# Attention weights transposed by VectorE and a round trip through DRAM instead of by TensorE

## The chip, the cores and the metric

The kernel runs on one core of a Trainium2 chip. The metric is the device time of one execution in microseconds; before the change it is 685.24 us, the median of three runs (685.07 to 685.33). TensorE is called PE in the profile, VectorE DVE, ScalarE ACT, GpSimd POOL; SP is the engine that issues most transfers (DMA).

## The reference

One encoder layer over 1024 tokens of width 1024, in float32. The normalised and modulated input `u` goes through one combined input projection; two groups of eight heads of width 64 mix the tokens, each with its own rule for the weights; their outputs are gated, concatenated and projected back, and a residual and a layer norm end it.

```python
# forgetting attention (FoX), blocks of 128 queries
s = jnp.einsum('bhqd,bhkd->bhqk', q, k) * scale
s = s + (f_q[..., :, None] - f_k[..., None, :])
p = jax.nn.softmax(jnp.where(causal, s, -jnp.inf), axis=-1)
out = jnp.einsum('bhqk,bhkd->bhqd', p, v)

# stick-breaking attention
z = jnp.einsum('bhqd,bhkd->bhqk', q, k) * scale
log_keep = jnp.where(strict, jax.nn.log_sigmoid(-z), 0.0)
later = lax.cumsum(log_keep, axis=3, reverse=True) - log_keep
w = jnp.where(strict, jnp.exp(jax.nn.log_sigmoid(z) + later), 0.0)
out = jnp.einsum('bhqk,bhkd->bhqd', w, v)

y = concat(y_fox * silu(fg), y_sb * silu(sg)) @ w_out
x = layer_norm(alpha * x + gate * y, ln_g, ln_b)
```

## The kernel before

**Units and pairs.** The 16 heads are worked in eight pairs of two; pairs 0 to 3 are stick-breaking, 4 to 7 forgetting. A unit is `(p, h, i)`: pair, head of the pair, block of 128 queries. Block `i` sees `i + 1` key blocks of 128, so a unit's weights are 128 by `(i + 1) * 128`, 4.5 blocks or 576 columns in the mean. There are 128 units. Stick-breaking pairs take the blocks in rising order, forgetting pairs in falling order, and pair 7 alternates between its heads.

**Precision.** Matrix products run on float32 values rounded to TensorE's shorter float32 type, with the rest of the rounding in a second tile ("hi" and "lo"). Each operand of a product so needs a cast (hi) and a subtraction (lo = full minus hi).

**A unit's way.** `att_scores` computes the scores S (lines 427, 428) into one PSUM tile of two banks, of which there is one. In a stick-breaking unit ScalarE makes two sigmoids of it (447: `kp`, 448: `be`), VectorE runs one or two scans backwards over `kp` (453, 457), and POOL multiplies `be` by the shifted `kp` (461) and clears the last column (462). In a forgetting unit VectorE adds the forget row `fb` and reduces (434), ScalarE takes the exponential with its sum (440), VectorE the reciprocal (441), and POOL scales the row (442). `att_transpose` then transposes each 128 by 128 block on TensorE by the identity into a PSUM tile `T` of up to four blocks (478), ScalarE casts that to hi (480) and VectorE subtracts for lo (481). `att_pv` multiplies the transposed weights with the values for two query blocks at once (493); its output goes through ScalarE, VectorE and POOL (512 to 514) and SP stores it to `y_dr` (522).

**What sets the order.** TensorE's order is written by hand: iteration `k` of the last loop issues the scores of unit `k`, a share of the fillers, the product of a pair of units that became ready in the iteration before, the transposes of unit `k - LAG` (LAG = 2), and another share of the fillers. The fillers are the input projections of later pairs (lines 270 to 272 and 327 to 329), and towards the end the output projection (882 to 884). The other engines, SP among them, are ordered by the framework's scheduler; each of them works strictly in its order, so an instruction that waits holds up all behind it.

**Buffers.** `att` has six tiles of 128 by 1024, shared by `kp`, `be`, `a` and the forget rows `fb`; a stick-breaking unit takes two, a forgetting unit one. The transposed weights have three tiles each for hi and lo. Keys lie in `kst` (hi, with a copy made by a transfer, line 252) and `klo`.

Of the kernel before, what the change touches and what calls it, by code (L numbers as in the profile page):

```python
# [8 lines left out]
F32 = mybir.dt.float32  # L9
F32R = mybir.dt.float32r  # L10
AF = mybir.ActivationFunctionType
ALU = mybir.AluOpType
# [15 lines left out]
def tile_hybrid_layer(  # L28
# [216 lines left out]
    def evac_k(p, ch, acc, kst, klo, heads):  # L245
        s = slice(ch * 512, ch * 512 + 512)
        for h in heads:
            r = slice(h * HD, h * HD + HD)
            o = slice((1 - h) * HD, (1 - h) * HD + HD)
            first = nc.scalar.copy(kst[h][r, s], acc[r, :])  # L250
            kf = kst[h].bitcast(F32)
            nc.sync.dma_start(kf[o, s], kf[r, s])
            if p not in CASTS_FIRST:
                last = nc.vector.tensor_tensor(klo[r, s], acc[r, :], kf[r, s], op=ALU.subtract)
        if p in CASTS_FIRST:
            for h in heads:
                r = slice(h * HD, h * HD + HD)
                last = nc.vector.tensor_tensor(klo[r, s], acc[r, :], kst[h].bitcast(F32)[r, s], op=ALU.subtract)  # L258
        return first, last
# [106 lines left out]
    def forget_rows(lf):  # L366
# [16 lines left out]
        nc.scalar.copy(fr, ft)  # L383
        nc.sync.dma_start(f_dr.rearrange("h (t p) -> (h t) p", p=P), fr)
        yield
# [21 lines left out]
    def att_causal(u):  # L407
        p, h, i = u
        if p >= 4:
            f = fb[2 * (p - 4) + h]  # L410
            dg = slice(i * P, i * P + P)
            nc.vector.tensor_tensor(f[:, dg], f[:, dg], ps_causal[0][:, :P] if ps_causal else causal, op=ALU.add)

    def att_scores(u, following):
# [3 lines left out]
        ns = 1 if ke <= 512 else 2  # L418
        w = ke // ns
        qs = slice(i * P, i * P + P)  # L420
        dg = slice(ke - P, ke)
        if p >= 4:
            f = fb[2 * (p - 4) + h]
        S = s_tile(f"S_{p}_{h}_{i}")
        for s in range(ns):
            ks = slice(s * w, s * w + w)
            nc.tensor.matmul(S[:, s, :w], qst[p][h][:, qs], kst[p][h][:, ks], start=True, stop=False)  # L427
            nc.tensor.matmul(S[:, s, :w], z, klo[p][:, ks], start=False, stop=True)  # L428
        v3 = lambda a: a[:, :ke].rearrange("p (a b) -> p a b", a=ns)
        if p >= 4:  # L430
            a = att_tile(f"a_{p}_{h}_{i}")
            nm = sb.tile([P, 1], F32, tag="nm", bufs=4, name=f"nm_{p}_{h}_{i}")
            l = sb.tile([P, 1], F32, tag="l", bufs=4, name=f"l_{p}_{h}_{i}")
            rows = nc.vector.tensor_tensor_reduce(out=v3(a), in0=S[:, :ns, :w], in1=v3(f),  # L434
                                           op0=ALU.add, op1=ALU.min, scale=-1.0, scalar=BIG,
# [5 lines left out]
            nc.vector.reciprocal(l, l)  # L441
            nc.gpsimd.tensor_scalar(a[:, :ke], a[:, :ke], l, 1.0, op0=ALU.mult, op1=ALU.mult)  # L442
            st_w[u] = a
        else:
# [16 lines left out]
            nc.gpsimd.tensor_tensor(be[:, :ke - 1], be[:, :ke - 1], kp[:, 1:ke], op=ALU.mult)  # L461
            nc.gpsimd.memset(be[:, ke - 1:ke], 0.0)
            st_w[u] = be

    def att_transpose(u):
# [639 lines left out]
```

## Time and profile before

| | before |
|---|---|
| device time, median of three | 685.24 us |
| profiled execution | 685.25 us |
| its span, first to last instruction | 683.5 us |
| busy PE / DVE / ACT / POOL | 98% / 66% / 56% / 63% |
| transfers | 81.60 MB, mean 119 GB/s |

A row of groups reads: line, engine, operation, tile written <- tiles read, shapes, count | total busy us, mean ns of one | idle us of the engine just before, and what ended it. A row of the timeline reads: start in us, duration in us, engine, line, operation. A row of transfers ends with KB each and the median us from issue to landing; the `SPq` rows of the timeline are the time for which SP is held by issuing one. A row of windows gives, for a stretch, busy us of PE, PE's weight loads, DVE, ACT and POOL with their counts, the granted clock, and the share and rate of the transfers.

### The profile page before, as it was taken

Reading aid. Unit: us, or ns where it says so; the run is one execution under the profiler, and the core shown is the slowest. Engines: PE = TensorE matmul, PEld = TensorE weight load, DVE = VectorE, ACT = ScalarE, POOL = GpSimd, SP = SyncE. Lnnn points to the kernel's source line nnn. Section 1 sums busy time; section 2 is a strip of 40 time slices with the busy share of each in tenths; the row PEclk is TensorE's granted clock in tenths of the full one; section 3 lists DMA queues with packets and bytes.
Section 4 is the critical chain, followed back from the end, with each engine's and each line's share of the span. In section 5 each row is a group of like instructions: output and inputs, shape, how many; then the busy total and the mean of one; then the engine's idle time right before and its main releaser. Section 6 shows DMA issues by size and latency. Waiting matters only on the chain.

```text
span 683.5 us, 11770 instructions
## 1 busy us (share of the span) xinstructions
PE 667.2 (98%) x4021; PEld 587.2 (86%) x4021; DVE 450.6 (66%) x914; ACT 382.0 (56%) x861; POOL 427.7 (63%) x558
## 2 busy tenths in 40 slices
PE   5999999999999999999999999999999999999995
PEld 4789898888998888889988888899988889888885
DVE  6785368867666667676675665765566677774645
ACT  5668357856567666566675564655565667531000
POOL 5558977756348566556388896877584364665411
PEclk9999999999999999999999999999999999999999
DMA  9966231112102121122144563453341298143301
GB/s 338 410 236 233 82 105 44 41 29 60 29 9 86 27 57 54 37 55 55 55 131 136 172 176 121 143 166 129 101 150 40 72 327 318 58 162 118 123 31 62
DMA packets 45036, 81.60 MB, mean 119 GB/s; under 512 B 5232, under 2 KB 18864, under 8 KB 44976
## 3 DMA queue, kind: packets, MB, share of 16 engines
q1 hardware_dynamic: 43536, 76.63, 33.8%
q10 hardware_dynamic: 1440, 4.21, 2.2%
q8 instruction: 32, 0.52, 0.3%
q14 instruction: 28, 0.23, 0.1%
HBM read 60.34 MB, written 16.29 MB: 112 GB/s over the span
## 4 chain that ended last, share of the span: by engine, by line
PE 94%; DMA 3%; DVE 2%; ACT 0%; issue 0%; POOL 0%; DVEq 0%
PE m L270 10%; PE m L272 10%; PE m L271 10%; PE pv L493 10%; PE T L478 9%; PE S L428 5%; PE S L427 5%; PE o L884 4%; PE o L882 4%; PE o L883 4%; PE v L327 4%; PE v L328 4%; PE v L329 4%; DMA raws<-in_w_qkg_dram 2%; PE st_late L589 1%; PE st_q L589 1%
## 5 line engine op out<-in xcount | busy, mean ns | idle before, releaser
L270 PE MATMUL m<-uh,whi 128*128 128x512 f32 x304 | 126.4, 416 | 0.0
L272 PE MATMUL m<-uh,wlo 128*128 128x512 f32 x304 | 119.7, 394 | 0.0
L271 PE MATMUL m<-ul,whi 128*128 128x512 f32 x304 | 119.7, 394 | 0.0
L481 DVE TENSOR_TENSOR pt<-T,pt 128x512 fp32r<-128x512 f32 (+2 forms) x192 | 100.5, 550 | 17.5 <-ACT pt L480 16.5
L461 POOL TENSOR_TENSOR be<-be,kp 128x127 f32<-128x127 f32 (+3 forms) x64 | 77.2, 1207 | 33.1 <-DVE kp L457 23.5
L480 ACT CAST pt<-T 128x512 fp32r<-128x512 f32 (+2 forms) x192 | 85.8, 480 | 16.1 <-PE T L478 12.5
L453 DVE TENSOR_TENSOR_SCAN kp<-kp,floor 128x512 f32<-128x512 f32 (+2 forms) x64 | 65.2, 1018 | 31.2 <-ACT kp L447 30.1
L493 PEld LDWEIGHTS pv<-pt,v 128*128 128x128 f32 (+1 forms) x640 | 77.1, 163 | 4.4 <-DVE pt L481 0.7
L493 PE MATMUL pv<-pt,v 128*128 128x256 f32 (+3 forms) x640 | 80.4, 271 | 0.5 <-DVE pt L481 0.5
L442 POOL TENSOR_SCALAR a<-a,l 128x1024 f32<-128x1024 f32 (+3 forms) x64 | 48.1, 751 | 40.3 <-DVE l L441 26.7
L272 PEld LDWEIGHTS m<-uh,wlo 128*128 128x128 f32 x304 | 57.1, 188 | 13.6
L440 ACT ACTIVATE a<-a,nm 128x1024 f32<-128x1024 f32 (+3 forms) x64 | 49.8, 778 | 33.8 <-DVE nm L434 32.7
L427 PE MATMUL S<-k,q 128*128 128x512 f32 (+5 forms) x192 | 66.5, 348 | 0.2 <-DVE nm L434 0.2
L428 PE MATMUL S<-kl,qz 128*128 128x512 f32 (+5 forms) x192 | 65.5, 342 | 0.0
L270 PEld LDWEIGHTS m<-uh,whi 128*128 128x128 f32 x304 | 57.3, 188 | 8.5 <-DVE kl L258 0.2
L271 PEld LDWEIGHTS m<-ul,whi 128*128 128x128 f32 x304 | 57.4, 189 | 8.0
L434 DVE CUSTOM_DVE_ANT_0 a<-S,fb 128x1024 f32<-128x1024 f32 (+3 forms) x64 | 48.3, 755 | 20.1 <-PE S L428 9.3
L514 POOL TENSOR_TENSOR ty<-ty,sg 64x256 f32<-64x256 f32 x64 | 47.5, 742 | 22.3 <-DVE ty L513 11.1
L447 ACT ACTIVATE kp<-S 128x128 f32<-128x128 f32 (+3 forms) x64 | 41.7, 652 | 31.6 <-PE S L428 29.4
L327 PE MATMUL v<-whi_v,uh 128*128 128x256 f32 (+1 forms) x192 | 56.0, 292 | 0.0
L405 ACT CAST qz<-q 64x128 fp32r<-64x128 f32 x128 | 37.4, 295 | 33.2 <-PE S L428 31.8
L328 PE MATMUL v<-whi_v,ul 128*128 128x256 f32 (+1 forms) x192 | 54.2, 282 | 0.0
(285 smaller groups left out, 1593.6 us busy)
## 6 DMA issues: line engine op xcount, KB each, us to landing
raw<-in_w_qkg_dram SPq DMA_DIRECT2D x38, 256.0 KB, 2.9
wss<-in_w_ss_dram SPq DMA_DIRECT2D x16, 512.0 KB, 8.4
x<-in_x_dram SPq DMA_DIRECT2D x8, 512.0 KB, 6.9
k<-k SPq DMA_DIRECT2D x32, 128.0 KB, 2.3
wg<-in_w_gate_dram SPq DMA_DIRECT2D x8, 512.0 KB, 4.9
raw_o<-in_w_out_dram SPq DMA_DIRECT2D x16, 256.0 KB, 2.8
fb<-f_dr ACTq DMA_DIRECT2D x8, 512.0 KB, 4.3
wo_dr<-whi_o SPq DMA_DIRECT2D x16, 256.0 KB, 2.5
```

The lines of the kernel that those rows point to most:

```text
L270: nc.tensor.matmul(acc, hi[:, c], u_hi[kt][:, s], start=(kt == 0), stop=False)
L271: nc.tensor.matmul(acc, hi[:, c], u_lo[kt][:, s], start=False, stop=False)
L272: nc.tensor.matmul(acc, lo[:, c], u_hi[kt][:, s], start=False, stop=(kt == NB - 1))
L327: nc.tensor.matmul(acc[:, :n], u_hi[kt][:, ts_], hi[:, s], start=(kt == 0), stop=False)
L328: nc.tensor.matmul(acc[:, :n], u_lo[kt][:, ts_], hi[:, s], start=False, stop=False)
L427: nc.tensor.matmul(S[:, s, :w], qst[p][h][:, qs], kst[p][h][:, ks], start=True, stop=False)
L428: nc.tensor.matmul(S[:, s, :w], z, klo[p][:, ks], start=False, stop=True)
L453: scan = nc.vector.tensor_tensor_scan(rv, rv, floor[0][:, 512 - n:][:, ::-1], initial=0.0, op0=ALU.mult, op1=ALU.max)
L461: nc.gpsimd.tensor_tensor(be[:, :ke - 1], be[:, :ke - 1], kp[:, 1:ke], op=ALU.mult)
L480: nc.scalar.copy(hi[:, :n, qo:qo + P], t3)
L481: nc.vector.tensor_tensor(lo[:, :n, qo:qo + P], t3, hi.bitcast(F32)[:, :n, qo:qo + P], op=ALU.subtract)
L493: nc.tensor.matmul(acc[:m, q0:256], vt[p][:, kb, h * P:h * P + m], pt[:, kb % 4, q0:], start=start, stop=stop)
```

## The change

All transposes of attention weights leave TensorE. In a stick-breaking unit, VectorE transposes the finished weights in squares of 32 by 32 into the other buffer (`kp`), with the column blocks regrouped by quarter; in a forgetting unit ScalarE, no longer POOL, scales the row and VectorE transposes in place. `through_dram` then writes the unit's 128 rows to a DRAM tile `far` (four of them) and reads it back in four transfers, one for each 32 destination partitions, which puts the squares in place. `att_transpose` keeps its two iterations of lag, and only casts (ScalarE) and subtracts from SBUF: on VectorE for the first four key blocks of stick-breaking units, on POOL for everything else.

For the forgetting pairs the key columns, the forget rows and the scores are kept in an order by quarters of 32 (`quartered`), so that the in-place transpose needs no regrouping: evacuations of keys write strided, the copy of the keys goes in pieces of 512 bytes, and the forget row is stored by eight transfers instead of one.

```diff
+    def by_blocks(t, n, natural):
+
+        return t[:, :n * P].rearrange("p (k s c) -> p k s c" if natural else "p (s k c) -> p k s c", k=n, s=4)
+
+    def on_dma(p):
+        return p >= 0
+
+    def quartered(p):
+
+        return p >= 4 and on_dma(p)
...
@@ att_scores, forgetting
-            nc.gpsimd.tensor_scalar(a[:, :ke], a[:, :ke], l, 1.0, op0=ALU.mult, op1=ALU.mult)
+            if moved:
+                nc.scalar.activation(a[:, :ke], a[:, :ke], AF.Copy, scale=l)
+                nc.vector.transpose(a[:, :ke], a[:, :ke])
+                through_dram(u, a, a)
...
@@ att_scores, stick-breaking
             nc.gpsimd.memset(be[:, ke - 1:ke], 0.0)
+            if moved:
+                nc.vector.transpose(by_blocks(kp, i + 1, False), by_blocks(be, i + 1, True))
+                through_dram(u, kp, be)
             st_w[u] = be
+
+    def through_dram(u, src, dst):
+
+        p, h, i = u
+        ke, run = (i + 1) * P, (i + 1) * 32
+        far = dr.tile([P, SEQ], F32, tag="far", bufs=4, name=f"far_{p}_{h}_{i}")
+        nc.sync.dma_start(far[:, :ke], src[:, :ke])
+        for s in range(4):
+            nc.sync.dma_start(dst[s * 32:s * 32 + 32, :ke].rearrange("k (q r) -> k q r", q=4),
+                              far[:, s * run:s * run + run].rearrange("(q k) r -> k q r", q=4))
...
@@ att_transpose
+            if on_dma(p):
+                full = a[:, :(i + 1) * P].rearrange("p (q k c) -> p k q c", q=4, c=32)[:, 4 * g:4 * g + n]
+                parts = [t[:, :n, qo:qo + P].rearrange("p k (q c) -> p k q c", q=4)
+                         for t in (hi, hi.bitcast(F32), lo)]
+                nc.scalar.copy(parts[0], full)
+                eng = nc.gpsimd if p >= 4 or g else nc.vector
+                eng.tensor_tensor(parts[2], full, parts[1], op=ALU.subtract)
+                continue
```

The order of the engines shows where the new work lies. First TensorE around the product of pair 1, head 0, blocks 6 and 7 (`pv_0_3`); the names give head and block, `v_3` is a piece of a value projection. Before:

```order
L329 MATMUL v_3_2164<-wlo_v_1_1963,uh_115 128x264
L493 MATMUL pv_0_3_2177<-pt_1_0_3_0_2064,v_514 128x256 x4
L493 MATMUL pv_0_3_2177<-pt_1_0_3_1_2073,v_514 128x256 x2
L493 MATMUL pv_0_3_2177<-pt_1_0_3_1_2073,v_514 128x128
L493 MATMUL pv_0_3_2177<-pt_1_0_3_0_2065,v_514 64x256 x4
L493 MATMUL pv_0_3_2177<-pt_1_0_3_1_2074,v_514 64x256 x2
L493 MATMUL pv_0_3_2177<-pt_1_0_3_1_2074,v_514 64x128
L493 MATMUL pv_0_3_2177<-pt_1_0_3_1_2074,v_514 64x256
L493 MATMUL pv_0_3_2177<-pt_1_0_3_1_2073,v_514 128x256
L478 MATMUL T_1_0_0_2201<-ident,be_1_0_2026 128x128
L327 MATMUL v_3_2164<-whi_v_2_1968,uh_116 128x264
```

And now:

```order
L354 MATMUL v_3_2209<-wlo_v_1_2014,uh_115 128x264
L567 MATMUL pv_0_3_2222<-pt_1_0_3_0_2114,v_514 128x256 x4
L567 MATMUL pv_0_3_2222<-pt_1_0_3_1_2118,v_514 128x256 x2
L567 MATMUL pv_0_3_2222<-pt_1_0_3_1_2118,v_514 128x128
L567 MATMUL pv_0_3_2222<-pt_1_0_3_0_2115,v_514 64x256 x4
L567 MATMUL pv_0_3_2222<-pt_1_0_3_1_2119,v_514 64x256 x2
L567 MATMUL pv_0_3_2222<-pt_1_0_3_1_2119,v_514 64x128
L567 MATMUL pv_0_3_2222<-pt_1_0_3_1_2119,v_514 64x256
L567 MATMUL pv_0_3_2222<-pt_1_0_3_1_2118,v_514 128x256
L352 MATMUL v_3_2209<-whi_v_2_2019,uh_116 128x264
```

The transposes (`T`) are gone, and all else keeps its place. Second, SP's queue at the same units (`raw` are weights, `k` the copies of keys, `y_dr` stores of head outputs). Before:

```order
L252 DMA k_1_1780<-k_1_1780 64x512
L522 DMA y_dr<-ty_0_1_1908 64x256
L121 DMA raw_0_0_2663<-in_w_qkg_dram 128x512
L522 DMA y_dr<-ty_0_2_2059 64x256
L522 DMA y_dr<-ty_0_3_2194 64x256
```

And now:

```order
L526 DMA far_0_6_1937<-kp_0_6_1928 128x896
L132 DMA raw_0_0_2714<-in_w_qkg_dram 128x512
L528 DMA be_0_6_1929<-far_0_6_1937 32x4x224 x4
L526 DMA far_0_7_1998<-kp_0_7_1989 128x1024
L526 DMA far_1_0_2076<-kp_1_0_2068 128x128
L596 DMA y_dr<-ty_0_2_2109 64x256
L528 DMA be_0_7_1990<-far_0_7_1998 32x4x256 x4
L528 DMA be_1_0_2069<-far_1_0_2076 32x4x32 x4
L526 DMA far_1_1_2150<-kp_1_1_2142 128x256
L526 DMA far_1_2_2202<-kp_1_2_2194 128x384
L528 DMA be_1_1_2143<-far_1_1_2150 32x4x64 x4
L528 DMA be_1_2_2195<-far_1_2_2202 32x4x96 x4
```

Each unit adds one write and four reads, and the loads and stores that were there stand between them; the whole queue grows from 294 transfers to 941. Third, SP's queue at the start of pair 7, where the output weights (`woh`, `wol`) are loaded, as it is now:

```order
L895 DMA woh_7048<-wo_dr 128x1024
L896 DMA wol_7049<-wo_dr 128x1024
L895 DMA woh_7081<-wo_dr 128x1024
L896 DMA wol_7082<-wo_dr 128x1024
L526 DMA far_0_6_7035<-a_0_6_7026 128x896
L895 DMA woh_7109<-wo_dr 128x1024
L896 DMA wol_7110<-wo_dr 128x1024
L933 DMA yr_4_7318<-y_dr 128x3x128
L528 DMA a_0_7_6962<-far_0_7_6971 32x4x256 x4
```

The reads of pair 7's first unit come behind those loads.

More of the change, by code (lines that the diff above doesn't have):

```diff
@@ L246, in evac_k, with made, home @@
         s = slice(ch * 512, ch * 512 + 512)
+        def made(t, r):
+            return t[r, :].rearrange("p (k s c) -> p k s c", k=4, s=4) if quartered(p) else t[r, :]
+        def home(t, r):
+            if not quartered(p):
+                return t[r, s]
+            return t[r, :].rearrange("p (s k c) -> p k s c", s=4, c=32)[:, 4 * ch:4 * ch + 4]
         for h in heads:
@@ L249, in evac_k @@
             o = slice((1 - h) * HD, (1 - h) * HD + HD)
-            first = nc.scalar.copy(kst[h][r, s], acc[r, :])
             kf = kst[h].bitcast(F32)
-            nc.sync.dma_start(kf[o, s], kf[r, s])
+            first = nc.scalar.copy(home(kst[h], r), made(acc, r))
+            if quartered(p):
+                both = [kf[x, :].rearrange("p (s z) -> p s z", s=4)[:, :, ch * P:ch * P + P] for x in (o, r)]
+                nc.sync.dma_start(*both)
+            else:
+                nc.sync.dma_start(kf[o, s], kf[r, s])
             if p not in CASTS_FIRST:
-                last = nc.vector.tensor_tensor(klo[r, s], acc[r, :], kf[r, s], op=ALU.subtract)
+                last = nc.vector.tensor_tensor(home(klo, r), made(acc, r), home(kf, r), op=ALU.subtract)
         if p in CASTS_FIRST:
@@ L383, in forget_rows @@
         nc.scalar.copy(fr, ft)
-        nc.sync.dma_start(f_dr.rearrange("h (t p) -> (h t) p", p=P), fr)
+        if quartered(4):
+            for hh in range(8):
+                nc.sync.dma_start(f_dr[hh].rearrange("(s t c) -> t s c", s=4, c=32),
+                                  fr[8 * hh:8 * hh + 8, :].rearrange("t (s c) -> t s c", s=4))
+        else:
+            nc.sync.dma_start(f_dr.rearrange("h (t p) -> (h t) p", p=P), fr)
         yield
```

31 lines of the change are left out of this document (26 added, 5 removed).

## The prediction

> **What bounds the kernel now.** I read the busy shares first, then the chain of waits, then the line of the scores, which shows the pace.
>
> ```profile
> PE 667.2 (98%) x4021; PEld 587.2 (86%) x4021; DVE 450.6 (66%) x914; ACT 382.0 (56%) x861; POOL 427.7 (63%) x558
> PE 94%; DMA 3%; DVE 2%; ACT 0%; issue 0%; POOL 0%; DVEq 0%
> by line: PE m L270 10.3%; PE m L272 10.2%; PE m L271 10.2%; PE pv L493 10.0%; PE T L478 9.1%; PE S L428 4.9%; PE S L427 4.9%; PE o L884 4.4%; PE o L882 4.4%; PE o L883 4.4%; PE v L327 4.2%; PE v L328 4.1%; PE v L329 4.1%; DMA raws<-in_w_qkg
> L427 PE MATMUL S<-k,q x192: 221/338/496, 88.8 to 610.7; 128*128 128x384 f32 x48, 128*128 128x512 f32 x48, 128*128 128x320 f32 x32, 128*128 128x448 f32 x32
> ```
>
> The chain is TensorE from end to end, and nothing makes it wait. The scores start at 88.8 us and the last unit's at 610.7 us, so the 128 units take 522 us, 4.08 us each. The sum below is made against the profiled execution, 685.25 us with a span of 683.5 us; the 1.75 us around the span stay, and the median of the runs is 685.24 us, the same.
>
> **What is removed.** The chain gives line 478, the 576 transposes, 9.1% of 683.5 us: 62.2 us, or 0.49 us for a unit. If nothing else came to wait, the kernel would take 685.25 - 62.2 = 623 us, and a unit 3.59 us.
>
> **How much time the new way may take.** TensorE's order is fixed: the product of a pair of units stands three units after the scores of the pair's second. The timeline shows it for one unit with eight key blocks (pair 1, head 0, block 7):
>
> ```profile
> 168.83 0.39 PE L428 MATMUL S<-kl,qz 128*128 128x512 f32 x1
> ...
> 169.54 1.03 ACT L447 ACTIVATE kp<-S 128x1024 f32<-128x1024 f32 x1
> ...
> 170.99 1.22 DVE L453 TENSOR_TENSOR_SCAN kp<-kp,floor 128x512 f32<-128x512 f32 x1
> ...
> 172.25 1.28 DVE L457 TENSOR_TENSOR_SCAN kp<-kp,floor 128x512 f32<-128x512 f32 x1
> ...
> 173.61 2.00 POOL L461 TENSOR_TENSOR be<-be,kp 128x1023 f32<-128x1023 f32 x1 [1.68 <-DVE kp L457]
> ...
> 179.54 1.04 PE L478 MATMUL T<-ident,be 128*128 128x128 f32 x8
> ...
> 183.70 1.94 PE L493 MATMUL pv<-pt,v 128*128 128x256 f32 x16
> ```
>
> From the end of the scores (169.2) to the product (183.7) are 14.5 us, of which the weights need 6.4 until POOL has multiplied them (175.6); 8.1 us are left, where the transposes, the casts and the subtractions now lie. Three units and the scores and projections of a fourth are some 3.3 units: 13.4 us at today's pace, 11.8 us at 3.59 us a unit. So the new way, from scores to product, may take 11.8 us for the whole gain and 13.4 us for no change; each us above that costs 128/3.3 = 39 us, since TensorE waits in order and the next scores stand behind the product.
>
> **The new way, step by step,** for the mean unit of 4.5 blocks (576 columns). The groups:
>
> ```profile
> L447 ACT ACTIVATE kp<-S 128x128 f32<-128x128 f32 (+3 forms) x64 | 41.7, 652 | 31.6 <-PE S L428 29.4 <-POOL fscratch L370 1.7
> L453 DVE TENSOR_TENSOR_SCAN kp<-kp,floor 128x512 f32<-128x512 f32 (+2 forms) x64 | 65.2, 1018 | 31.2 <-ACT kp L447 30.1 <-issue 0.2
> L457 DVE TENSOR_TENSOR_SCAN kp<-kp,floor 128x128 f32<-128x128 f32 (+3 forms) x32 | 28.2, 880 | 1.1
> L461 POOL TENSOR_TENSOR be<-be,kp 128x127 f32<-128x127 f32 (+3 forms) x64 | 77.2, 1207 | 33.1 <-DVE kp L457 23.5
> L434 DVE CUSTOM_DVE_ANT_0 a<-S,fb 128x1024 f32<-128x1024 f32 (+3 forms) x64 | 48.3, 755 | 20.1 <-PE S L428 9.3
> L440 ACT ACTIVATE a<-a,nm 128x1024 f32<-128x1024 f32 (+3 forms) x64 | 49.8, 778 | 33.8 <-DVE nm L434 32.7
> L442 POOL TENSOR_SCALAR a<-a,l 128x1024 f32<-128x1024 f32 (+3 forms) x64 | 48.1, 751 | 40.3 <-DVE l L441 26.7
> L481 DVE TENSOR_TENSOR pt<-T,pt 128x512 fp32r<-128x512 f32 x96 | 64.6, 686 | 16.8 <-ACT pt L480 16.3
> L480 ACT CAST pt<-T 128x512 fp32r<-128x512 f32 x96 | 54.8, 587 | 7.7 <-PE T L478 5.0
> L126 POOL TENSOR_TENSOR wlo<-raw,whi 128x512 fp32r<-128x512 f32 x38 | 49.1, 1297 | 2.4 <-DMA wo_dr<-wlo_o 0.8
> y_dr<-ty SPq DMA_DIRECT2D x56, 64.0 KB, 1.9
> wo_dr<-whi_o SPq DMA_DIRECT2D x16, 256.0 KB, 2.5
> yr<-y_dr SPq DMA_DIRECT2D x8, 256.0 KB, 3.4
> 171.92 0.33 SPq L121 DMA_DIRECT2D raw<-in_w_qkg_dram  x1
> 248.72 0.45 SPq L522 DMA_DIRECT2D y_dr<-ty  x1
> 346.00:611.00 265.00, 264.74 (x1617) 233.84 (x1615) 174.57 (x451) 152.53 (x375) 185.16 (x215) 1.00 0.46 149
> ```
>
> 1. To the finished weights, stick-breaking: sigmoid 0.65, scans (65.2 + 28.2)/64 = 1.46, product 1.21, together 3.3 us; forgetting: 0.76 + 0.78 and ScalarE's new scaling (L440 is the nearest row) 0.78, together 2.3 us. The unit above took 0.9 us more than its four operations. I take 4.0; 3.3 is the least, 4.9 the most (once more 0.9).
> 2. Transpose on VectorE: not in the trace. 686 ns per 512 columns gives 0.75 us; at least that, at most twice. I take 0.75, since L481 moves as many bytes.
> 3. Write to DRAM (mean 295 KB): between 1.9 and 2.5 us to landing; I take 2.3, near the 256 KB row. SP must see it land before it may issue the reads, and behind them on SP stand weight loads (POOL splits them one projection ahead), key copies, stores of head outputs and the next unit's write.
> 4. Four reads: an issue holds SP 0.33 to 0.45 us; with 0.45 the fourth starts 1.35 us after the first. It lands 1.9 us later at the least, 3.4 us at the most (the row that reads 512-byte pieces back); a read has a quarter of the unit's bytes, so 2.2. In the forgetting half the transfer engines are 46% busy with 149 GB/s (last row above, pairs 4 to 7), and the round trip adds 2 x 295 KB x 64 units in 265 us, 142 GB/s: there they come near full, which is why I stay above 1.9.
> 5. Cast and subtraction: the last subtraction follows its cast. On VectorE 0.59 + 0.69, on POOL 0.59 + 1.30 for 512 columns; the two groups of a longer unit overlap in part. I take 1.8. Behind a late cast on ScalarE stand the fourth next unit's sigmoids and the evacuations of projections.
> 6. Waits for engines that do something else: VectorE 66%, ScalarE 56%, POOL 63% busy, and SP in order; five visits at 0.5 us are 2.5. At least 0.5 in all, at most 4.5.
>
> Sum: 4.0 + 0.75 + 2.3 + 1.35 + 2.2 + 1.8 + 2.5 = 14.9 us. Over 3.3 that is 4.52 us a unit, 0.44 above today's: 128 x 0.44 = +56 us. The ends: 3.3 + 0.75 + 1.9 + 1.0 + 1.9 + 1.3 + 0.5 = 10.7 us (TensorE sets the pace, 623) and 4.9 + 1.5 + 2.5 + 1.35 + 3.4 + 1.9 + 4.5 = 20 us (6.1 us a unit, 940).
>
> The mean hides who waits. A unit of eight blocks needs 6.4 + 1.2 + 2.5 + 1.35 + 2.2 + 2.5 + 2.5 = 18.7 us against 14.5 now, so the products of a head's long pairs stall; short ones fit. The six weight buffers hold three stick-breaking units, so a unit's second sigmoid waits for the subtraction of the third before it: the same sum plus 0.65 us over four units, 3.9, which is looser than 4.52.
>
> The Trainium skill, "DMA: Bandwidth & Descriptors" (Anatomy of one DMA), puts a transfer at about 2.0 us fixed plus its bytes at 436 GB/s. That is fitted to transfers issued by GpSimd, and the 64 KB row here, 1.9 us, is 0.25 below it. By the page the write would take 2.7 and a read 2.2, the sum grow by 0.4 us and the time by 16 us.
>
> **One place more.** In pair 7 the reads stand behind loads of the output weights:
>
> ```profile
> woh<-wo_dr SPq DMA_DIRECT2D x8, 512.0 KB, 8.2
> wol<-wo_dr SPq DMA_DIRECT2D x8, 512.0 KB, 7.7
> SPq L522 <- POOL ty L514: 164.2, 44, 9.9
> ```
>
> A read that shares the transfer engines with these lands some 6 us late, once to the first products of the pair: +6. Key copies in 512-byte pieces and the forget row in eight small stores lie far ahead of their readers: 0, since projections run beside them; if not, 2 us once.
>
> **Forecast:** 685.25 + 56 + 6 = 747 us, slower. Of its own, with waits of 1.5 to 4 us in step 6, 708 to 805.
>
> **The rivals.**
> A, the other side: the round trip is hidden. TensorE never waits if the sum stays under 11.8 us, and under 13.4 us the kernel gains. For it: the steps without waits sum to 12.4, SP is mostly idle today, and fewer casts from PSUM compete. With waits of 0 to 0.5 us the sum is 12.4 to 12.9, a unit 3.83 us: -32 + 6 gives 659 us. Against it: the long units, whose slack the short ones cannot lend, and pair 0, which has half the projections of the others to fill the time.
> B, SP becomes the bound. Per unit it issues one write, waits until it has landed (2.3), issues four reads (1.8), and about 220 other transfers come in between (0.4 each, 0.7 a unit): 4.8 us if nothing overlaps, 128 x 0.72 = +92, 777 us; and where SP sits in front of a store of the head output (row above: 164 us of such waits, harmless today), the next unit's write is late too, up to 5.2 us a unit, 828. For it: the queue holds 941 transfers instead of 294. Against it: the order puts some writes two ahead of the reads and weight loads into the gaps.
> C, POOL in the forgetting half. It gains 96 subtractions of 36,864 columns in all at 2.53 ns: +93, and loses 48: 185 + 45 = 230 of 265 us, still under. Only if the 32-column pieces cost double (+186 - 48 = 323) does it bind there: +58, 743 us.
> D, the gain and the stalls cancel within 0.2%: a sum of 13.4.
>
> **How the numbers follow.** Forecast 0.57, B 0.21, A 0.12, C 0.05, D 0.03, other slower ways 0.02. The range reaches from between A and the forecast's lower end, 670, to B's upper, 830. Faster by over 0.2% 0.12 (A), same 0.03 (D), slower 0.85; 0.2% is what this kernel's runs can tell from no change.
>
> **What would show it.** Right: TensorE's busy share falls to 80 to 85%, the chain passes through SP, transfers and the casts, idle time of TensorE stands before the product and names the split (cast or subtraction), most of it in pairs of blocks 6, 7 and 4, 5, while the pace from first to last scores is 4.4 to 4.7 us. For B, SP's queue has no idle time and its waits for its own write's landing are the largest. For A the pace is under 4 us and TensorE stays over 95%. Step 2 fails if a transpose of 1,024 columns takes over 2 us; steps 3 and 4 if landings differ much from 2.3 and 2.2; step 5 if POOL's 512-column subtraction is far from 1.3 us. The forecast is wrong in its mechanism if TensorE does not wait before the products.

## The result, and the profile after

The changed kernel takes 840.27 us, the median of four runs (836.96 to 842.34), against 685.20: a ratio of 1.226 (95% interval 1.222 to 1.230). The direction was foretold, the size was not: 747 us, at most 830. The profiled execution took 842.34 us with a span of 840.6. The lines that answer to those of before are, from the page (busy times, the granted clock by slices, the chain of waits), from the view of line 472 (the scores: shortest, median and longest in ns, first and last start in us), and from TensorE's waits (us in total, times, longest):

```profile
PE 669.6 (80%) x3445; PEld 563.4 (67%) x3445; DVE 502.9 (60%) x914; ACT 432.1 (51%) x925; POOL 510.3 (61%) x622
PEclk9999987999987989989899989899979895899999
DMA 30%; PE 29%; DVE 10%; SPq 8%; POOL 8%; ACT 8%; issue 6%; ACTq 0%; DVEq 0%; POOLq 0%
L472 PE MATMUL S<-k,q x192: 221/361/793, 90.0 to 768.3; 128*128 128x384 f32 x48, 128*128 128x512 f32 x48, 128*128 128x320 f32 x32, 128*128 128x448 f32 x32
PE pv L567 <- ACT pt L545: 96.6, 30, 25.6
PE S L472 <- ACT be L501: 20.8, 10, 8.2
PE pv L567 <- DVE pt L547: 12.9, 11, 2.8
PE S L472 <- DVE nm L482: 9.7, 8, 1.8
```

The scores now take from 90.0 to 768.3 us, 678 us instead of 522: 5.30 us a unit for 4.08. What comes after the last scores is the same length as before (840.6 - 768.3 = 72.3 us, 683.5 - 610.7 = 72.8), so the whole loss of 156 us is in the units. TensorE is idle for 840.6 - 669.6 = 171 us, against 16. Its busy time did not fall although 62 us of transposes went: the same matmuls take 670 us in place of 667 - 62 = 605, at a mean granted clock of 0.911 in place of 0.999.

The same unit as in the prediction (pair 1, head 0, block 7), from the timelines of five engines; a bracket gives the idle time before a row and what ended it:

```profile
197.63 0.39 PE L473 MATMUL S<-kl,qz 128*128 128x512 f32 x1
198.27 0.82 ACT L545 CAST pt<-be 128x512 fp32r<-128x512 f32 x2 [1.84 <-DMA be<-far]
199.12 1.18 ACT L271 CAST k<-m 64x512 fp32r<-64x512 f32 x2
200.33 1.02 ACT L500 ACTIVATE kp<-S 128x1024 f32<-128x1024 f32 x1
201.89 1.02 ACT L501 ACTIVATE be<-S 128x1024 f32<-128x1024 f32 x1 [0.36 <-DMA far<-kp]
202.97 0.33 PE L472 MATMUL S<-k,q 128*128 128x128 f32 x1 [2.04 <-ACT be L501]
204.22 1.27 DVE L510 TENSOR_TENSOR_SCAN kp<-kp,floor 128x512 f32<-128x512 f32 x1
205.57 2.00 POOL L514 TENSOR_TENSOR be<-be,kp 128x1023 f32<-128x1023 f32 x1 [2.50 <-DVE kp L510]
208.04 1.42 DVE L517 STREAM_TRANSPOSE kp<-be 128x1024 f32<-128x1024 f32 x2
209.34 0.81 SPq L526 DMA_DIRECT2D far<-kp  x2
212.39 3.64 SPq L528 DMA_DIRECT2D be<-far  x8
216.82 1.34 ACT L545 CAST pt<-be 128x512 fp32r<-128x512 f32 x3 [1.01 <-DMA be<-far]
217.49 1.57 PE L567 MATMUL pv<-pt,v 128*128 128x256 f32 x11 [1.61 <-ACT pt L545]
```

The scores end at 198.0 us and the unit's product begins at 217.5: 19.5 us, where the kernel before took 14.5. The first loss of this unit stands at its very start. ScalarE's sigmoid begins only at 200.3: in ScalarE's order the casts of an earlier unit and key evacuations stand ahead of it, and ScalarE had been idle for 1.84 us until those casts' read had landed. The scores of the next unit wait for this unit's second sigmoid (202.97), since there is one score tile, and that sigmoid had waited 0.36 us more for a buffer. In this unit a late read so makes the next unit's scores late, not only its own product. It is not a mean unit: over the 64 stick-breaking units the first sigmoid begins 0.70 us after the scores, and 0.14 us in the kernel before.

The new operations by shape, and the transfers of the longest units of both kinds (`kp` and `be` are stick-breaking, `a` forgetting):

```profile
L517 DVE STREAM_TRANSPOSE kp<-be 128x1024 f32<-128x1024 f32 x8 | 9.8, 1228 | 0.0
L547 POOL TENSOR_TENSOR pt<-a,pt 128x512 fp32r<-128x512 f32 x48 | 61.4, 1285 | 30.1 <-ACT pt L545 27.1 <-DMA y_dr<-ty 1.8 <-PE S L473 0.5
L547 DVE TENSOR_TENSOR pt<-be,pt 128x512 fp32r<-128x512 f32 x40 | 44.5, 1114 | 33.2 <-ACT pt L545 32.7
far<-kp SPq DMA_DIRECT2D x8, 512.0 KB, 2.9
be<-far SPq DMA_DIRECT2D x32, 128.0 KB, 2.9
far<-a SPq DMA_DIRECT2D x8, 512.0 KB, 5.4
a<-far SPq DMA_DIRECT2D x32, 128.0 KB, 3.8
```

VectorE's squares and POOL's subtraction cost what was foretold (1.23 us for 1,024 columns, 1.29 us for 512). VectorE's own subtraction does not: 1.11 us for 512 columns, where it took 0.69 from PSUM. The transfers of the forgetting half are slower than those of the other half: there (419 to 768 us) the transfer engines are 72% busy, in the stick-breaking half (90 to 419 us) 51%.

### The profile page after: what moved, and what is told of

It is laid out like the page before. It is cut to its first block, busy times and chain, and to the rows that moved or that the text cites. A ratio compares the mean times of both kernels' runs of the same rounds, so it can differ in the third digit from the quotient of the medians.

```text
span 840.6 us, 12309 instructions
## 1 busy us (share of the span) xinstructions
PE 669.6 (80%) x3445; PEld 563.4 (67%) x3445; DVE 502.9 (60%) x914; ACT 432.1 (51%) x925; POOL 510.3 (61%) x622
## 4 chain that ended last, share of the span: by engine, by line
DMA 30%; PE 29%; DVE 10%; SPq 8%; POOL 8%; ACT 8%; issue 6%; ACTq 0%; DVEq 0%; POOLq 0%
DMA a<-far 8%; SPq L528 7%; DMA be<-far 6%; DMA far<-a 5%; PE pv L567 4%; DMA far<-kp 4%; PE o L956 3%; PE o L957 3%; ACT pt L545 3%; PE o L958 3%; POOL pt L547 3%; DVE pt L547 2%; DVE kp L506 2%; PE m L295 2%; PE m L297 2%
## 5 line engine op out<-in xcount | busy, mean ns | idle before, releaser
L567 PE MATMUL pv<-pt,v 128*128 128x256 f32 (+3 forms) x640 | 111.7, 324 | 118.9 <-ACT pt L545 96.6
L567 PEld LDWEIGHTS pv<-pt,v 128*128 128x128 f32 (+1 forms) x640 | 94.5, 199 | 139.8 <-ACT pt L545 108.5
L547 POOL TENSOR_TENSOR pt<-a,pt 128x512 fp32r<-128x512 f32 (+1 forms) x96 | 95.6, 1010 | 54.5 <-ACT pt L545 46.2
L296 PE MATMUL m<-ul,whi 128*128 128x512 f32 x304 | 124.4, 409 | 0.0
L545 ACT CAST pt<-a 128x512 fp32r<-128x512 f32 (+1 forms) x96 | 46.2, 510 | 95.3 <-DMA a<-far 95.2
L547 DVE TENSOR_TENSOR pt<-be,pt 128x512 fp32r<-128x512 f32 (+2 forms) x64 | 62.2, 971 | 40.1 <-ACT pt L545 39.1
L545 ACT CAST pt<-be 128x512 fp32r<-128x512 f32 (+2 forms) x96 | 45.8, 511 | 61.9 <-DMA be<-far 58.0
L472 PEld LDWEIGHTS S<-k,q 128*128 128x128 f32 x192 | 38.1, 199 | 47.4 <-ACT be L501 25.2
L492 DVE STREAM_TRANSPOSE a<-a 128x1024 f32<-128x1024 f32 (+3 forms) x64 | 49.6, 776 | 33.4 <-ACT a L491 33.1
L482 DVE CUSTOM_DVE_ANT_1 a<-S,fb 128x896 f32<-128x896 f32 (+6 forms) x56 | 38.5, 687 | 43.8 <-POOL pt L547 13.7
```

What stands on the lines that cost most here:

```text
L296: nc.tensor.matmul(acc, hi[:, c], u_lo[kt][:, s], start=False, stop=False)
L472: nc.tensor.matmul(sp, qst[p][h][:, qs], kh, start=True, stop=False)
L545: nc.scalar.copy(parts[0], full)
L547: eng.tensor_tensor(parts[2], full, parts[1], op=ALU.subtract)
L567: nc.tensor.matmul(acc[:m, q0:256], vt[p][:, kb, h * P:h * P + m], pt[:, kb % 4, q0:], start=start, stop=stop)
```

## The experiments

All are edits of the changed kernel unless said otherwise; times are medians, ratios are to the kernel before (685.1 to 685.3 us beside each).

**The round trip as a whole, and three of its four reads.** First neither write nor reads, so the squares stay where VectorE put them:

```diff
-                through_dram(u, a, a)
...
-                through_dram(u, kp, be)
-            st_w[u] = be
+            st_w[u] = kp
```

> The write to DRAM and the four reads are left out, so the 32 by 32 squares stay where VectorE put them; VectorE's transposes, the casts, the subtractions on POOL and VectorE and the scaling on ScalarE all stay. Theory: the way loses write (2.6), four reads (3.8) and SP's waits (2.0), 8.4 us, and is 8.8 us long, under the 11.8 us that 3.3 units take at TensorE's own pace: TensorE no longer waits, its clock is back at 1.00, and the time is 625 to 650 us. Rival (POOL or another engine is full with the moved work): 720 us or more.

704.29 us, 1.028 (1.025 to 1.031). The trip costs 136 us. But even without it the kernel is 19 us slower than before, and some 80 above the floor of 623, between what the two theories gave. Then only the first read of four (`range(4)` to `range(1)`; three quarters of the rows stay unplaced):

> Only the first of the four reads is left, so three quarters of each unit's squares stay unplaced. Theory: the way loses the three further issues (1.47 us) and some 0.2 us of landing, 1.7 us of 17.2: pace 5.34 to 4.8 us, 68 us less, about 770 us. Rival (SP's queue is the bound): SP loses three issues of 0.46 us a unit and most of the bytes read, 1.4 us of 5.34 a unit, 177 us less, about 660 us.

798.83 us, 1.166 (1.164 to 1.168). Three of four reads are worth 41 us, less than the theory's 68 and far from the rival's 177, so SP's queue is part of the way and not the bound.

**A longer distance from scores to product.** `LAG = 2` becomes 3, and then 4:

> The casts and products of a unit stand one unit later in the order (LAG 3 instead of 2), nothing else changes. Theory (the length of the way from scores to product, 17.2 us here, over its distance of 3.23 units sets the pace): the distance becomes 4.23 units, so the pace falls from 5.34 to 4.1 us a unit if the way keeps its length, 128 x 1.27 = 163 us less, about 677 us; up to 740 if six weight buffers make the sigmoids wait for the write of an earlier unit. Rival (SP's queue, the transfer engines or POOL are full): the same work in the same queues, so the pace and the time stay, 830 to 850 us.

> The changed kernel with LAG 4 in place of 2: the product follows the scores by two units more. LAG 3 took 818 us. Theory (from LAG 3 on the six weight buffers set the pace: a stick-breaking unit holds two of them until its subtraction, so three units are in flight, and 16.4 us / 3 = 5.5 us a unit, whatever the distance of the product): 810 to 830 us. Rival (the distance still counts, each unit of it as the first one): 818 - 22 = 796 us, down to 780.

818.1 us, 1.194 (1.191 to 1.197), and 828.44 us, 1.209 (1.207 to 1.211). A sum of 17 us spread over 4.3 units instead of 3.3 should have hidden most of the wait; it gave 22 us, and one unit more took back 10. TensorE's idle time before products falls from 118 us to 13 with LAG 3 and to nothing with LAG 4. Its largest waits with LAG 3:

```profile
PE S L472 <- DVE nm L482: 49.6, 18, 14.0
PE S L472 <- ACT be L501: 45.5, 27, 7.1
```

The wait has moved from the product to the scores. So the distance to the product is one loop, and another, which makes the scores themselves late, lies right behind it. The 828 us with LAG 4 lie where the weight buffers would put them; whether it is the buffers, the next two runs were to tell. A seventh weight buffer with LAG 3, paid for by one tile less in the ring of projection weights:

```diff
-        return big("att", 6, name, dt)
+        return big("att", 7, name, dt)
...
-    RING = 5
+    RING = 4
```

> LAG 3 and a seventh weight buffer; the room comes from one of the five places of the ring of split projection weights. Theory: if buffers held the run with LAG 3 back, this one is faster than it by 10 to 60 us and comes near 680; if only the distance counts, both are the same within 10 us. Rival (full queues): 830 to 850 as well.

829.14 us, 1.210 (1.206 to 1.214), 11 us more than LAG 3 alone; TensorE now waits for projection weights too, so it says little of the buffer. Half the buffers for the short stick-breaking units, with LAG 3 and the ring as it was:

```diff
+            if i < 4:
+                both = att_tile(f"kb_{p}_{h}_{i}")
+                kp, be = both[:, :512], both[:, 512:]
...
```

> The changed kernel with LAG 3 (818 us), and the stick-breaking units of one to four key blocks keep both of their arrays (up to 512 columns each) in one of the six buffers, where they took two. Theory (from LAG 3 on the six buffers set the pace, three units in flight): the 32 short units are then held by the distance alone, 16.4 / 4.3 = 3.8 us in place of some 5, 785 us, 775 to 800. Rival (ScalarE's order, the casts that wait for reads ahead of later sigmoids, sets it): 810 to 820 us.

815.01 us, 1.190 (1.187 to 1.193): 3 us, and the single runs of both kernels overlap. For these units the buffers are not what holds the pace; for the long ones and the forgetting half the run says nothing.

**Do casts that wait for a read make the loss?** The stick-breaking pairs alone on the new way (`on_dma` is `p < 4`), and then the same transfers with casts and subtractions that read VectorE's squares and wait for no read:

```diff
-            st_w[u] = be
+            st_w[u] = kp if moved else be
```

> The changed kernel with the new way in the four stick-breaking pairs alone; the forgetting pairs keep their transposes on TensorE, their key order and POOL's scaling. In the changed kernel the four pairs took 328 us against 258 before. Theory (each half's loss is its own): 685 + 70 = 755 us, 745 to 765. Rival (the loss of the second half is a late start handed on from the first): 790 us or more; or (the first half's loss comes from transfers that the second half prepares) 720 us or less.

> As the kernel with the stick-breaking pairs alone on the new way, with the same write and four reads into the same buffers, but casts and subtractions read the squares from the buffer that VectorE transposed into, so that no engine waits for a read to land except through the reuse of a buffer; the attention weights of these pairs are wrong. Theory (the casts that wait for the reads, in ScalarE's and TensorE's fixed order, are the loss): as the kernel without a round trip in these pairs, where they took 268 us against 258 before: 690 to 705 us. Rival (the buffers are the loss: a read holds its buffer until it has landed, some 14 us behind the scores, and three units share six buffers): 735 to 755 us.

765.54 us, 1.117 (1.115 to 1.119), and 714.43 us, 1.042 (1.040 to 1.043). Of 80 us lost by this half, 51 go with the wait of the casts, with every transfer still there. TensorE's waits show where: before products it waits 47 us in the first run and not at all in the second; before scores the wait for ScalarE does not shrink. The first three rows are the first run's, the next two the second's, where ScalarE in part waits for buffers that a read holds:

```profile
PE pv L567 <- ACT pt L545: 34.6, 18, 4.9
PE S L472 <- ACT be L501: 22.7, 11, 8.3
PE pv L567 <- DVE pt L547: 9.9, 13, 2.1
PE S L472 <- ACT be L501: 35.1, 18, 6.3
ACT be L501 <- DMA be<-far: 13.2, 15, 2.0
```

The stick-breaking half's loss is its own: from the first scores of pair 0 to those of pair 4 this half takes 331 us alone, 329 in the changed kernel and 258 before. The forgetting half was not run alone.

**Is the lower clock a cost of its own?** Eight transposes of the identity for each unit, into a tile that nobody reads, where the old transposes stood:

```diff
+            warm = t_tile(f"warm_{p}_{h}_{i}")
+            for b in range(8):
+                nc.tensor.transpose(warm[:, b % 4 * P:b % 4 * P + P], ident, ident)
```

> The changed kernel with eight extra transposes of the identity on TensorE for each unit, into a PSUM tile that nobody reads, at the place in TensorE's order where the old transposes stood. Nothing else changes. A group of eight takes 1.04 us in the kernel before, so 128 of them are 133 us of matmul time. Theory (the way from scores to product sets the pace, TensorE waits in 171 us of the span): the extra work lies in time that TensorE waited, 830 to 855 us, TensorE's busy share rises from 80 to about 95%, and the granted clock, 0.91 before, rises above 0.95. Rival 1 (the lower clock that follows the stalls is itself on the path; it makes the matmuls of the changed kernel 65 us longer, 670 against 667 - 62 = 605 us): with the clock back, 840 - 65 = 775 us, up to 800. Rival 2 (TensorE's own work sets the pace): 840 + 133 = 973 us.

867.75 us, 1.264 (1.260 to 1.269), clock 0.946.

```profile
PE 759.5 (88%) x4469; PEld 663.6 (77%) x4469; DVE 494.9 (57%) x914; ACT 432.4 (50%) x925; POOL 511.5 (59%) x622
```

The time lies 13 us above the theory's range and far from both rivals. TensorE is busy 90 us longer and the span only 25.5 (866.1 for 840.6), so TensorE's own work is mostly hidden in the waits. A clock nearer full speed did not bring the 65 us of the first rival back; what little it may have brought cannot be told from the cost of the added work.

**POOL's share.** All subtractions on VectorE, with and without the round trip:

```diff
-                eng = nc.gpsimd if p >= 4 or g else nc.vector
+                eng = nc.vector
```

> The changed kernel with all 96 subtractions of the split on VectorE, none on POOL. Theory (POOL's slower subtraction ends the way of every forgetting unit and of the long stick-breaking units, and POOL's two-input work holds VectorE's): a 512-column subtraction 0.69 us in place of 1.29 takes about 0.5 us from the mean way of 17.2 us, at 39 us of time for each us 20 us, and VectorE's mean, 1.11 us for 512 columns, falls towards 0.69: 800 to 825 us. Rival (VectorE, with 40 us more work, is now late with scans, transposes and row sums): 840 us or more.

> Leaves out the write to DRAM and the four reads, as the earlier kernel without the round trip (704 us), so the squares stay where VectorE put them and the attention weights are wrong; and all 96 subtractions are on VectorE. Theory (in 704 us TensorE waits about 25 us for POOL, by name, and for VectorE held by POOL): 665 to 690 us, TensorE busy over 93%. Rival (VectorE, 71% busy already, becomes the bound, the scores wait for its row sums and scans): 700 us or more.

853.89 us, 1.246 (1.243 to 1.249), 14 us worse; and 702.77 us, 1.026 (1.022 to 1.030), the same as with POOL. Both went against the theory: in these two kernels nothing is gained by moving the subtractions from POOL to VectorE. VectorE is then busy 566 us in place of 503 with the round trip, so the runs do not price POOL's part alone.

**Distance without the trip.** LAG 3 and no round trip:

> Leaves out the write to DRAM and the four reads (704 us without more), so the attention weights are wrong, and lets the product follow the scores by one unit more (LAG 3 in place of 2). Theory (what is left above the floor of 623 us is still waiting in a fixed order, which one more unit of distance loosens): 640 to 680 us, TensorE busy over 94%. Rival (VectorE and POOL are late with the scores' own work, sigmoids, scans, products, row sums, and hold the single score tile, however far behind the product stands): 695 to 710 us.

701.47 us, 1.024 (1.022 to 1.025). Here TensorE waits for sigmoids (15.2 us) and row sums (9.2 us) before scores, not for products.

**What is left above 623.** No trip, and no squares on VectorE either:

```diff
-                nc.vector.transpose(a[:, :ke], a[:, :ke])
...
-                nc.vector.transpose(by_blocks(kp, i + 1, False), by_blocks(be, i + 1, True))
```

> Leaves out the round trip (704 us) and VectorE's transposes too: casts and subtractions read the weights as they are, so the attention weights are wrong. What is left of the change is ScalarE's scaling, the split from SBUF and its place on POOL, and TensorE without transposes. Theory (VectorE's 98 us of squares stand in front of scans, row sums and subtractions and make them late): 645 to 675 us, TensorE busy over 94%. Rival (the split from SBUF, with POOL's subtractions and two-input work on VectorE and POOL at once, is what remains): 690 us or more. Floor without any wait: 623 us.

682.24 us, 0.995 (0.994 to 0.996): the squares are 22 us, and the rest of the gain is still missing. With all subtractions on VectorE besides, and the kernel *before* with its transposes alone left out:

> As the kernel without round trip and squares (682 us; its attention weights are untransposed and so wrong), with all 96 subtractions on VectorE, none on POOL. Theory (POOL, 76% busy and late by name before products and projections, is what held the 682 us): 640 to 660 us. Rival (VectorE's subtractions from two SBUF operands, 0.96 us in place of 0.69 where POOL runs beside them, only move the wait): 672 to 690 us.

```diff
-            for b in range(n):
-                kb = 4 * g + b
-                nc.tensor.transpose(tp[:, b * P:(b + 1) * P], a[:, kb * P:(kb + 1) * P], ident)
-            t3 = tp[:, :n * P].rearrange("p (a b) -> p a b", a=n)
+            t3 = a[:, 4 * g * P:(4 * g + n) * P].rearrange("p (a b) -> p a b", a=n)
```

> The kernel before with TensorE's transposes alone left out: casts and subtractions read the untransposed weights from SBUF, on ScalarE and VectorE as before, POOL scales as before (the attention weights are wrong). Theory (the prediction's floor holds when nothing else moves): 685 - 62 = 623 us, up to 635. Rival (TensorE was not alone: other engines' ways, sigmoids to scans to products, set a bound close behind it): 650 us or more, and then the prize of the whole change was less than half of what the prediction counted.

670.9 us, 0.981 (0.977 to 0.985; the four runs lie between 665 and 675), and 678.7 us, 0.991 (0.989 to 0.993). The prediction's floor is not reached once the split reads SBUF: leaving 62 us of transposes out brings 6.5. The last pair asks whether the source does it. Both are the kernel before with one transpose per group of up to four blocks; in the first the split reads that block from PSUM as often as four, in the second it reads SBUF.

```diff
+            nc.tensor.transpose(tp[:, :P], a[:, 4 * g * P:(4 * g + 1) * P], ident)
+            t3 = tp[:, :P].unsqueeze(1).to_broadcast([P, n, P])
```

> The kernel before with one transpose in each group of up to four blocks, 192 in place of 576; ScalarE's cast and VectorE's subtraction read that one block from PSUM as often as they read four (so the other blocks' weights are wrong), in the same sizes as before. 384 transposes are 62.2 x 384 / 576 = 41.5 us of TensorE. Theory (what TensorE gives up is gained as long as the split reads PSUM): 685 - 41.5 = 644 us, up to 655. Rival (another bound lies close behind TensorE, wherever the split reads): 668 us or more.

> As the kernel with one transpose in each group, but the cast and the subtraction read the untransposed weights from SBUF and nobody reads the transposed block (the attention weights are wrong). Theory (two SBUF operands on VectorE beside POOL's work cost both engines): 675 to 695 us, VectorE's 512-column subtraction over 0.9 us against 0.69. Rival (the source makes no difference): within 5 us of the run from PSUM.

652.74 us, 0.954 (0.952 to 0.956), and 690.82 us, 1.008 (1.007 to 1.010). From PSUM, 41.5 us of transposes less bring 33; from SBUF they bring nothing. Moving the split's source costs 38 us. Their rows, first from PSUM, with TensorE's busy time:

```profile
L479 DVE TENSOR_TENSOR pt<-T,pt 128x512 fp32r<-128x512 f32 x96 | 64.5, 686 | 12.6 <-ACT pt L478 11.2
PE 630.3 (97%) x3637; PEld 545.9 (84%) x3637; DVE 447.5 (69%) x914; ACT 380.4 (58%) x861; POOL 426.6 (66%) x558
```

Then from SBUF, with TensorE's largest waits, ScalarE's waits for POOL before casts, and the longest of these subtractions beside POOL's rows of that time:

```profile
L479 DVE TENSOR_TENSOR pt<-a,pt 128x512 fp32r<-128x512 f32 x48 | 51.9, 1090 | 14.8 <-ACT pt L478 14.0 <-PE pv L491 0.6
PE S L427 <- DVE nm L434: 13.6, 11, 4.8
PE S L427 <- ACT be L448: 7.4, 8, 2.1
ACT pt L478 <- POOL a L442: 46.8, 40, 2.5
ACT pt L478 <- POOL be L461: 21.8, 19, 2.4
308.31 4.07 DVE L479 TENSOR_TENSOR pt<-be,pt 128x512 fp32r<-128x512 f32 x1
308.03 0.61 POOL L125 TENSOR_SCALAR whi<-raw 128x512 fp32r<-128x512 f32 x1
308.61 1.99 POOL L461 TENSOR_TENSOR be<-be,kp 128x1023 f32<-128x1023 f32 x1
310.57 1.26 POOL L126 TENSOR_TENSOR wlo<-raw,whi 128x512 fp32r<-128x512 f32 x1
```

From PSUM the 512-column subtraction takes 686 ns whatever POOL does: 89 of the 96 overlap a row of POOL and 7 do not, and both sorts take 686 ns in the mean. From SBUF the 18 that overlap none take 686 ns too, and the 78 that do take 1.15 us. The one shown takes 4.07: POOL's rows stand back to back until 311.8 us and the subtraction ends 0.55 us later. What stands behind it on VectorE, row sums and scans among it, is held meanwhile.

A second thing changes with the source. From PSUM a cast waits for TensorE's transposes, and in 62 of the 64 stick-breaking units it stands in ScalarE's order behind the sigmoids of two later units. From SBUF it needs only POOL's result, and in 54 of the 64 units it stands behind the sigmoids of one later unit or of none. ScalarE then waits 76 us for POOL before casts, where it waited 11 us for transposes. The 38 us are the price of both together; how they divide was not measured.

**Only the units that should fit.** The kernel before, with the stick-breaking units of one to four key blocks alone on the new way:

```diff
-    def on_dma(p):
-        return p >= 0
+    def on_dma(p, i=0):
+        return p < 4 and i < 4
```

> The kernel before, except that only the stick-breaking units of one to four key blocks take the new way; all other units keep their transposes on TensorE. 80 of the 576 blocks move: 62.2 x 80 / 576 = 8.6 us less on TensorE. Theory (a unit gains where its way, 12.3 to 13.1 us from scores to the end of the cast in the changed kernel, stays under 13.4 us less what waits; these units stay mostly under it, and with few transfers on SP the waits shrink): 677 to 683 us, faster than the kernel before. Rival (the waits follow the round trip itself and not its load; each head's one-block unit comes behind the long units of the head before and is late with them): 685 to 700 us.

709.9 us, 1.035 (1.034 to 1.037). It loses as well: 15 of the 25 us in pair 0 (62.3 us from its first sigmoid to the next pair's, 47.1 before), which has half the projections of pairs 1 to 5 to fill the time. No version that kept the new way beat the kernel before.

## Why the prediction was wrong in size

**One ladder of the time**, each step from one run to the next:

| | us | step |
|---|---|---|
| before | 685.2 | |
| transposes out, split from SBUF on ScalarE and VectorE | 678.7 | -6.5 |
| scaling on ScalarE, key order by quarters, most subtractions on POOL | 682.2 | +3.5 |
| VectorE's squares | 704.3 | +22 |
| the write and one read | 798.8 | +95 |
| three more reads | 840.3 | +41 |

**The way from scores to product, term by term.** The measured values are means over the second units of the 64 pairs of blocks, whose scores open the way, in the trace of after. A landing is the last signal of the transfer's semaphore, counted from the start of the issue, as in the rows from which the prediction took its prices.

| step | foretold, us | measured, us |
|---|---|---|
| 1, to finished weights | 4.0 (at most 4.9) | 5.13 |
| 2, squares | 0.75 | 0.77 |
| 3, write to landing | 2.3 (at most 2.5) | 2.88 |
| 4, four issues, last landing | 1.35 + 2.2 | 1.46 + 2.78 |
| 5, first cast to product | 1.8 | 1.91 |
| 6, waits between | 2.5 (at most 4.5) | 2.30 |
| sum: scores of the second unit to product | 14.9 | 17.2 |

**Steps 1, 3 and 4 were priced too low**, by 1.1, 0.6 and 0.7 us, and the first two came out beyond their upper bounds; steps 2, 5 and 6 came as foretold.

Step 1 was added up from busy times and the gaps of one unit. Over all 128 units it is 5.35 us, and in the kernel before it was 4.42 already (stick-breaking 3.98, forgetting 4.85, where POOL began to scale 2.2 us after the exponential). The other 0.9 us came with the change, and not from ScalarE alone: in stick-breaking units the gap before the first sigmoid grew by 0.56 us, that before the scans by 0.35 and that before POOL's product by 0.28; in forgetting units VectorE begins the row sum 1.46 us after the scores, for 0.28 before.

Steps 3 and 4 took their prices from transfers of the kernel before. Over these second units, the write of the stick-breaking half lands after 2.56 us and the last read after 2.60; in the forgetting half, which the prediction saw coming near full, after 3.20 and 2.97.

**The path failed too.** The prediction divided the sum by 3.3 units to get the pace. That 17.2 us over 5.30 us a unit are 3.25 is no proof that the way sets the pace, since TensorE's fixed order makes it so whatever it waits for: the kernel before, where no product waits, has 12.95 over 4.08, or 3.2; LAG 3 has 22.3 over 5.12, or 4.35; LAG 4 has 27.0 over 5.19, or 5.2. So 747 us plus 2.3 us at 39 each, 837, meets the measured time by the order alone. The test is the distance. With LAG 4 no product waits any more, and a unit still takes 5.19 us. The loop through the buffers and the scores, which the prediction put at 3.9 us a unit and called looser than 4.52, or another loop that ends before the scores, is by then nearly as tight as the whole kernel's 5.30. The wait before the products, which the prediction had as the one cost, is worth some 22 us as long as that second loop stands.

What a cast that waits for a read costs was shown for one half. Casts that wait for no read, with the products where they were and all transfers in place, take the stick-breaking half from 331 us to 286. Products farther off take it from 329 to 310 with LAG 3 and to 311 with LAG 4. So a waiting cast costs more than the wait of its own product. The prediction said, without a price, that sigmoids stand behind a late cast on ScalarE. That this is the path of the rest is likely but not shown: the way to the finished weights of this half is 5.65 us with waiting casts and 5.64 without.

**The floor of 623 failed as well.** Step 5 took the subtraction from SBUF at the price of L481, which reads PSUM, and step 2 and the floor assumed that nothing else would slow. Moving the source costs 38 us, which is more than half of the prize. The Trainium skill, "SBUF — State Buffer" (Who interferes with whom), says that a VectorE instruction with two SBUF inputs contends with a GpSimd instruction that reads SBUF, that one with at most one SBUF input, outside the two-port modes, does not, and that the shared port pair is an exclusive lock. The trace agrees: 686 ns from PSUM with or without POOL, and from SBUF 686 ns without POOL and 1.15 us beside it. This rule spoke against the change and the prediction did not weigh it.

**The write** took 3.03 us for 295 KB in the mean of all 128 units, 2.56 in the stick-breaking half and 3.51 in the forgetting half. An estimate by the rule of the Trainium skill that the prediction weighed against its rows, "DMA: Bandwidth & Descriptors" (Anatomy of one DMA), is 2.7: the trace agrees to 0.15 us in the first half and not in the second.

**The rivals.** A, hidden: refuted by the time, and even the short units alone lose. B, SP as the bound: refuted as the whole, since three reads fewer bring 41 us and SP is held by issues for 370 of the 678 us of the units; but SP's landings and issues are on the chain (SPq 8%, DMA 30%), as foretold, and its largest waits are for its own write's landing (60 and 47 us), which was B's sign. C, POOL in the forgetting half: its condition did not hold, since the pieces cost 1.29 us for 512 columns as priced and POOL is busy 228 of 349 us there. D did not happen.

**What was to show it.** TensorE busy 80%, idle before products that wait for casts, 76 of 118 us of it before blocks 6 and 7, and a chain through SP, transfers and casts came as foretold; the pace, 5.30, lies outside 4.4 to 4.7. Pair 7 lost most, 36 us against 9 to 23 of the others, counted from first scores to first scores; what of it is the output weights' loads was not measured.

**What stays open.** Why LAG 3 and LAG 4 bring so little. In the forgetting half VectorE's row sums are named, and they in part wait for a buffer that POOL's subtraction holds; in the stick-breaking half ScalarE's sigmoid. Which of ScalarE's order, the one score tile and the buffers of the long units is last was not separated. Nor is it known what the 11 us are that the kernel without squares gains by having its subtractions on VectorE (682 to 671), when the same move with squares brings nothing.

## What to carry to other kernels

The time that leaves the bounding engine is a prize only if the next loop leaves room, so measure that first with the work simply left out; here 62 us of transposes were worth 6.5 once their reader had moved from PSUM to SBUF. Where a fixed order sets the distance between two steps, the length of the way over the pace gives that distance whatever the limit is; only a run with another distance tells whether the way sets the pace. An operand's place is part of an instruction's price: look for POOL's reads beside every VectorE instruction with two SBUF inputs. When an in-order engine gets an instruction that waits for a transfer, price what stands behind it, not only the instruction's own reader.

## What the runs showed of the hardware

The granted clock of TensorE falls, roughly, with its idle time: 0.999 with 16 us idle, 0.970 with 52 (the transposes left out), 0.943 with 85 (the stick-breaking pairs alone), 0.946 with 107 (idle time filled with transposes) and 0.911 with 171. The products, which stand right behind the stalls, take 324 ns in the mean in place of 271 (L493 before):

```profile
L567 PE MATMUL pv<-pt,v 128*128 128x256 f32 (+3 forms) x640 | 111.7, 324 | 118.9 <-ACT pt L545 96.6 <-DVE pt L547 12.9 <-POOL pt L547 8.6
```

The Trainium skill, "TensorE: Matmul & The Clock Gate" (Part 1), has the array fall to half its clock after an idle window of some 3.4 us. The stalls here are up to 25.6 us long, and the trace agrees in direction. Busy time of TensorE is therefore no measure of its work across such kernels: 605 and 670 us here for the same matmuls.
